# Storing the first tile of a row softmax as two DMAs of eight rows instead of one of sixteen

## The chip, the core and the metric

The kernel runs on one core of a Trainium2 chip. The metric is device time in microseconds (us), the median of several executions. Lower is better.

## The reference

The input x has shape (16, 1024, 512) in float32. For every row of 512 values the kernel computes a softmax at temperature 0.5:

```python
x_scaled = x / 0.5
x_max = np.max(x_scaled, axis=-1, keepdims=True)
exp_x = np.exp(x_scaled - x_max)
out = exp_x / np.sum(exp_x, axis=-1, keepdims=True)
```

There are 16,384 rows, 33.55 MB in and 33.55 MB out.

## The kernel before

The rows are cut into eight tiles ("chunks", c = 0 to 7). A tile has 128 partitions with G = 16 rows of 512 floats each, which is 4 MiB. A partition's 16 rows lie next to each other in HBM, so a DMA of a whole tile is 128 runs of 32 KiB. Six tile buffers exist (BUFS = 6). Tiles 6 and 7 reuse the buffers of tiles 0 and 1, so their loads wait until the stores of tiles 0 and 1 have landed.

All work on a tile is done in place, by blocks of rows that the table BLOCKS lists: tile 0 in blocks of 4, 4 and 8 rows, tiles 1 to 6 whole, tile 7 in two blocks of 8. That makes 11 blocks. For each block:

- shift (L74, L78): VectorE (DVE) takes each row's negated maximum and doubles it, which gives the bias. When the tile has no load yet, this step first issues it (L66) on SyncE's DMA queue (SP). LOADS cuts tile 0's load into 4 and 12 rows; the other tiles are loaded whole.
- exponentials (L85): ScalarE (ACT) computes exp(2x + bias), one instruction per row, and adds up the row's sum.
- scale_vector (L100, L102): DVE takes the reciprocal of the sums and multiplies seven eighths of the block's rows.
- scale_scalar (L111): ACT multiplies the remaining rows.
- store (L119): ACT's queue issues the DMA to HBM. STORES lists the row ranges of each tile's store, and a range is issued with the block whose end is the range's end. Before, every tile is stored whole, after its last block.

The order is written out by hand. The main loop is:

```python
    for i in range(n):
        if i + 1 < n:
            exponentials(i + 1)
        scale_vector(i)
        scale_scalar(i)
        if i + 2 < n:
            shift(i + 2)
        store(i)
```

Two DMA queues carry everything: q1 takes the loads, issued by SP, and q10 takes the stores, issued by ACT. Each DMA is spread over the same 16 DMA engines, eight partitions to each, so one tile's load or store is eight packets of 32 KiB on each engine, and each engine then writes a 4-byte packet for the semaphore. The framework gives the DMAs eight completion semaphores in turn.

Of the kernel before, what the change touches and what calls it, by code (L numbers as in the profile page):

```python
# [1 line left out]

# [4 lines left out]


@with_exitstack
def kernel(  # L10
    ctx: ExitStack,
    tc: tile.TileContext,
    x: bass.AP,
    out: bass.AP,
):
    nc = tc.nc
    fp32 = mybir.dt.float32
    P = nc.NUM_PARTITIONS
    AX = mybir.AxisListType.X
    EXP = mybir.ActivationFunctionType.Exp  # L20
    COPY = mybir.ActivationFunctionType.Copy
    MAX = mybir.AluOpType.max

    D = x.shape[-1]
    xf = x.flatten_outer_dims()
    of = out.flatten_outer_dims()
    N = xf.shape[0]

    G = 16
    C = N // (P * G)
    assert C * P * G == N
    xr = xf.rearrange("(c p g) d -> c p g d", p=P, g=G)
    outr = of.rearrange("(c p g) d -> c p g d", p=P, g=G)
    WHOLE = [(0, G)]
    LOADS = [[(0, 4), (4, G)]] + [WHOLE] * 7
    BLOCKS = [[(0, 4), (4, 8), (8, G)]] + [WHOLE] * 6 + [[(0, 8), (8, G)]]
    STORES = [WHOLE] * 8  # L40
    BMAX = 16
    BUFS = 6

    data = ctx.enter_context(tc.tile_pool(name="data", bufs=BUFS))
    stats = ctx.enter_context(tc.tile_pool(name="stats", bufs=6))

    ctx.enter_context(tc.manual_schedule())


    warm = stats.tile([P, 1], fp32, name="warm", bufs=1)  # L50
    nc.vector.memset(warm, 0.0)  # L51
    nc.scalar.activation(out=warm, in_=warm, func=EXP)  # L52

    chunks = {}
    blocks = [(c, lo, hi) for c in range(C) for lo, hi in BLOCKS[c]]
    n = len(blocks)
    biases, sums, recips = {}, {}, {}

    def load(c):
        if c < BUFS:  # L60
            chunks[c] = data.tile([P, G, D], fp32, name="xt")
        else:
            chunks[c] = chunks[c - BUFS]
        xt = chunks[c]
        for lo, hi in LOADS[c]:
            nc.sync.dma_start(out=xt[:, lo:hi, :], in_=xr[c][:, lo:hi, :])  # L66

    def shift(i):
        c, lo, hi = blocks[i]
        if c not in chunks:  # L70
            load(c)
        b = hi - lo
        negmax = stats.tile([P, BMAX], fp32, name="negmax")
        nc.vector.tensor_reduce(  # L74
            negmax[:, 0:b], chunks[c][:, lo:hi, :], axis=AX, op=MAX, negate=True
        )
        biases[i] = stats.tile([P, BMAX], fp32, name="bias")
        nc.vector.tensor_scalar_mul(biases[i][:, 0:b], negmax[:, 0:b], 2.0)  # L78

    def exponentials(i):  # L80
        c, lo, hi = blocks[i]
        sums[i] = stats.tile([P, BMAX], fp32, name="sums")
        for g in range(hi - lo):
            row = chunks[c][:, lo + g, :]
            nc.scalar.activation(  # L85
                out=row,
                in_=row,
                func=EXP,
                bias=biases[i][:, g : g + 1],
                scale=2.0,  # L90
                accum_out=sums[i][:, g : g + 1],
            )


    def scale_vector(i):
        c, lo, hi = blocks[i]
        b = hi - lo
        k = b - b // 8
        recips[i] = stats.tile([P, BMAX], fp32, name="recip")
        nc.vector.reciprocal(recips[i][:, 0:b], sums[i][:, 0:b])  # L100
        rows = chunks[c][:, lo : lo + k, :]
        nc.vector.tensor_mul(  # L102
            rows, rows, recips[i][:, 0:k].unsqueeze(2).broadcast_to((P, k, D))
        )

    def scale_scalar(i):
        c, lo, hi = blocks[i]
        b = hi - lo
        for g in range(b - b // 8, b):
            row = chunks[c][:, lo + g, :]  # L110
            nc.scalar.activation(  # L111
                out=row, in_=row, func=COPY, scale=recips[i][:, g : g + 1]
            )

    def store(i):
        c, _, end = blocks[i]
        for lo, hi in STORES[c]:
            if hi == end:
                nc.scalar.dma_start(  # L119
                    out=outr[c][:, lo:hi, :], in_=chunks[c][:, lo:hi, :]  # L120
                )

    shift(0)
    shift(1)
    exponentials(0)
# [10 lines that stand above are left out]
# [1 line left out]
_INS = ['x']  # L137
_OUTS = [((16, 1024, 512), 'float32')]


# [23 lines left out]
```

## Time and profile before

| | us |
|---|---|
| median of 5 runs (162.13 to 162.39) | 162.27 |
| the profiled execution, whole | 162.43 |
| its span in the profile | 160.7 |
| DVE busy | 134.6 |
| ACT busy | 102.1 |
| share of the 16 DMA engines' span: q1 (loads) | 49.3% |
| the same: q10 (stores) | 48.4% |

The span runs from the first to the last recorded event of the execution; 1.7 us of the profiled execution's time lie outside it. A queue's share counts the time that its packets took, summed over the 16 engines, against 16 spans. The names L66, L85 and so on are line numbers of the kernel before; the store's line is L119 before and L120 in the changed kernel.

### The profile page before, as it was taken

To read this page: it belongs to the slowest core of one execution; us is meant where nothing else is said; L and a number is where in the kernel's file an instruction comes from. 1 tells how busy PE (TensorE), PEld (TensorE's weight loads), DVE (VectorE), ACT (ScalarE), POOL (GpSimd) and SP (SyncE) were. 2 spreads that over 40 slices of the span, in tenths; PEclk is the share of its full clock that TensorE was granted. 3 is DMA by queue.
4 is the path that set the end of the run, shared out by engine and by line. 5 is a ranking of instruction groups with operands and counts; after the bars stand their busy time and mean duration, and the time that the engine had idled before them with its cause. 6 is when DMAs were issued, how large, how long until landed. Compare 5 with 4: busy or idle time off the path is not lost.

```text
span 160.7 us, 402 instructions
## 1 busy us (share of the span) xinstructions
DVE 134.6 (84%) x45; ACT 102.1 (64%) x273; POOL 0.2 (0%) x4
## 2 busy tenths in 40 slices
DVE  0608999999999999999999999999999999956000
ACT  3072549069979963997299909990999890790000
POOL 0000000000000000000000000000000000000000
DMA  5999999999999999999999999999999999999993
GB/s 192 461 441 473 392 408 506 392 392 516 392 400 383 400 449 457 400 441 465 400 432 465 408 408 483 408 400 490 416 392 490 424 392 457 457 392 449 465 392 139
DMA packets 2450, 67.13 MB, mean 418 GB/s; under 512 B 272, under 2 KB 272, under 8 KB 272
## 3 DMA queue, kind: packets, MB, share of 16 engines
q1 hardware_dynamic: 1296, 33.56, 49.3%
q10 hardware_dynamic: 1152, 33.55, 48.4%
q14 instruction: 2, 0.02, 0.0%
HBM read 33.55 MB, written 33.55 MB: 418 GB/s over the span
## 4 chain that ended last, share of the span: by engine, by line
DVE 80%; DMA 7%; ACT 4%; issue 0%; SPq 0%
DVE negmax L74 42%; DVE xt L102 36%; DMA xt<-in_x_dram 7%; ACT xt L85 4%; DVE bias L78 1%; DVE recip L100 1%; SPq L66 0%
## 5 line engine op out<-in xcount | busy, mean ns | idle before, releaser
L85 ACT ACTIVATE xt<-xt,bias 128x512 f32<-128x512 f32 x128 | 90.4, 707 | 41.5 <-DVE bias L78 41.0
L74 DVE TENSOR_REDUCE negmax<-xt 128x16 f32<-128x8192 f32 (+2 forms) x11 | 69.9, 6353 | 9.3 <-DMA xt<-in_x_dram 9.3
L102 DVE TENSOR_TENSOR xt<-xt,recip 128x7168 f32<-128x7168 f32 (+2 forms) x11 | 62.0, 5637 | 0.4
L85 ACT ACTIVATION_READ_ACCUMULATOR xt<-xt,bias 128x1 f32 x128 | 23.9, 187 | 0.0
L111 ACT ACTIVATE xt<-xt,recip 128x512 f32<-128x512 f32 x15 | 9.9, 706 | 0.0
L100 DVE RECIPROCAL recip<-sums 128x16 f32<-128x16 f32 (+2 forms) x11 | 2.4, 218 | 1.8 <-ACT xt L85 1.8
L78 DVE TENSOR_SCALAR bias<-negmax 128x16 f32<-128x16 f32 (+2 forms) x11 | 1.9, 173 | 0.4
L52 ACT ACT_TABLE_LOAD x1 | 1.3, 1283 | 0.7 <-PEq L148 0.7
L51 DVE MEMSET warm<- 128x1 f32 x1 | 0.1, 59 | 0.8 <-PEq L148 0.8
L52 ACT ACTIVATE warm<-warm 128x1 f32<-128x1 f32 x1 | 0.2, 202 | 0.0
L148 POOL MEMSET const-bfloat16-1.0<- 128x1 bf16 x1 | 0.1, 101 | 0.0
L148 POOL MEMSET const-uint8-127<- 128x1 uint8 x1 | 0.1, 101 | 0.0
L148 POOL MEMSET const-float32-0.0<- 128x1 f32 x1 | 0.1, 98 | 0.2 <-issue 0.2
L148 POOL MEMSET const-float32-1.0<- 128x1 f32 x1 | 0.1, 98 | 0.0
## 6 DMA issues: line engine op xcount, KB each, us to landing
out_dram<-xt ACTq DMA_DIRECT2D x8, 4096.0 KB, 23.1
xt<-in_x_dram SPq DMA_DIRECT2D x7, 4096.0 KB, 30.0
xt<-in_x_dram SPq DMA_DIRECT2D x1, 3072.0 KB, 11.5
xt<-in_x_dram SPq DMA_DIRECT2D x1, 1024.0 KB, 4.6
```

What stands on the lines that cost most here:

```text
L51: nc.vector.memset(warm, 0.0)
L52: nc.scalar.activation(out=warm, in_=warm, func=EXP)
L74: nc.vector.tensor_reduce(negmax[:, 0:b], chunks[c][:, lo:hi, :], axis=AX, op=MAX, negate=True)
L78: nc.vector.tensor_scalar_mul(biases[i][:, 0:b], negmax[:, 0:b], 2.0)
L85: nc.scalar.activation(out=row, in_=row, func=EXP, bias=biases[i][:, g : g + 1], scale=2.0, accum_out=sums[i][:, g : g + 1],)
L100: nc.vector.reciprocal(recips[i][:, 0:b], sums[i][:, 0:b])
L102: nc.vector.tensor_mul(rows, rows, recips[i][:, 0:k].unsqueeze(2).broadcast_to((P, k, D)))
L111: nc.scalar.activation(out=row, in_=row, func=COPY, scale=recips[i][:, g : g + 1])
L148: nc = _bacc.Bacc("TRN2", target_bir_lowering=False, num_devices=1)
```

## The change

Tile 0's entry in STORES becomes two ranges of eight rows. The function store now returns unless the block is the tile's last one, and then issues all of the tile's ranges one after the other. For tiles 1 to 7 nothing changes. Tile 0's store was one DMA with 128 runs of 32 KiB; it becomes two DMAs on the same queue, each with 128 runs of 16 KiB.

```diff
-    STORES = [WHOLE] * 8
+    STORES = [[(0, 8), (8, G)]] + [WHOLE] * 7
...
     def store(i):
         c, _, end = blocks[i]
+        if end < G:
+            return
         for lo, hi in STORES[c]:
-            if hi == end:
-                nc.scalar.dma_start(
-                    out=outr[c][:, lo:hi, :], in_=chunks[c][:, lo:hi, :]
-                )
+            nc.scalar.dma_start(
+                out=outr[c][:, lo:hi, :], in_=chunks[c][:, lo:hi, :]
+            )
```

## The prediction

> **What bounds the kernel now.** I read the page first: the busy shares, the DMA rows and the traffic by slices.
>
> ```profile
> span 160.7 us, 402 instructions
> DVE 134.6 (84%) x45; ACT 102.1 (64%) x273; POOL 0.2 (0%) x4
> DMA  5999999999999999999999999999999999999993
> q1 hardware_dynamic: 1296, 33.56, 49.3%
> q10 hardware_dynamic: 1152, 33.55, 48.4%
> ```
>
> The chain of waits names DVE for 80% of the span, and DVE is busy for 84%. But the two DMA queues together fill 97.7% of the time of all 16 DMA engines. Nothing there can be idle for long, whatever the chain says. So I went to the trace's packet records (start, duration, size of each). On every engine the packets stand end to end from the first at 1.74 us to the last, with no gap over 0.19 us except where the instruction queue puts in a packet. Fifteen engines end between 158.1 and 158.6; one, which also carried two 8 KiB instruction fetches, ends at 159.45, and the last store lands right after it. The kernel is bound by DMA time from end to end. What the engines compute matters only when it makes a queue run dry.
>
> Next I asked for the traffic of stretches around tile 0's store: before it, at its start, beside the loads, and when only stores are left.
>
> ```profile
> DMA packets 297, 8.66 MB, mean 433 GB/s; under 512 B 32, under 2 KB 32, under 8 KB 32
> ...
> DMA packets 48, 1.57 MB, mean 384 GB/s; under 512 B 0, under 2 KB 0, under 8 KB 0
> q1 hardware_dynamic: 32, 1.05, 82.2%
> q10 hardware_dynamic: 16, 0.52, 29.6%
> ...
> DMA packets 291, 8.49 MB, mean 424 GB/s; under 512 B 32, under 2 KB 32, under 8 KB 32
> q1 hardware_dynamic: 147, 4.29, 49.7%
> q10 hardware_dynamic: 144, 4.19, 48.6%
> ...
> DMA packets 440, 12.85 MB, mean 428 GB/s; under 512 B 48, under 2 KB 48, under 8 KB 48
> ```
>
> These are 26 to 46 us, 46.9 to 51, 51 to 71 and 116 to 146. The rate is 424 to 433 GB/s everywhere but in the second stretch. There the queues hold 111.8% of the stretch for 48 packets: the 32 load packets are slow. In the records a 32 KiB packet takes 1213 ns all through the run. When the store queue comes alive, two load packets on each engine take 1.4 to 2.1 us instead, each engine at its own moment. Summed over the two, the excess is 0.78 to 1.15 us per engine, mean 0.945. It happens at no other store or load: after 49.6 us neither queue is ever dry until the loads end, so no other DMA meets a queue that has to start.
>
> The third stretch shows how the two queues share an engine: about one packet each. In the records they alternate strictly, and even the 4-byte semaphore packet takes a turn.
>
> Last, the issues and the waits of the load queue.
>
> ```profile
> 44.65 0.71 ACT L111 ACTIVATE xt<-xt,recip 128x512 f32<-128x512 f32 x1
> 45.39 0.37 ACTq L119 DMA_DIRECT2D out_dram<-xt  x1
> 46.20 0.72 ACT L85 ACTIVATE xt<-xt,bias 128x512 f32<-128x512 f32 x1 [0.84 <-DVE bias L78]
> ...
> 147.35 0.34 ACTq L119 DMA_DIRECT2D out_dram<-xt  x1
> ...
> SPq L66 <- DMA out_dram<-xt: 75.6, 2, 56.7
> ```
>
> The store is issued in a hole of ACT's, and load 6 waits 56.7 us for tile 0's store to land, until 69.4 us.
>
> **The change part by part.** *Issue.* One more DMA on ACT's queue costs 0.34 to 0.37 us there. In the built program the first half waits for nothing (ACT has long seen its rows done), so it can go at about 44.7, under the L111 that the second half waits for. Even were it to follow, 45.39 + 0.37 + 0.34 = 46.10 is short of 46.20, when ACT's next exponential gets its bias. Queued behind it is that exponential alone; cost nothing. Without that hole it would be 0.37 us of ACT, which has 4 to 6 us of idle time per tile. DVE's order does not change.
>
> *Semaphores.* The extra DMA shifts the turn of the eight semaphores. Load 5, which was issued at once, now waits for load 0's first part. That lands at 5.4 us, with some 20 MB still queued ahead of load 5; nothing runs dry. Store 3 waits for the first half of store 0 and store 7 for store 1, both landed long before. Load 6 waits for both halves, load 7 for store 1 as before.
>
> *Packets.* 8 KiB, 24 KiB and 32 KiB packets take 309, 912 and 1213 ns: 37.7 ns per KiB and 8 ns fixed. A 16 KiB packet is then 610 ns, and two are 8 ns more than one of 32 KiB. Eight pairs on each engine plus one more semaphore packet of 9 ns: +0.07 us, on the path in full, as the engines have no gap. The Trainium skill, "DMA: Bandwidth & Descriptors", section on the anatomy of one DMA, speaks against the change: it gives each DMA a fixed cost of about 2.0 us beside its bytes. No such cost shows here: store follows store on q10, and the 24 KiB packets follow the 8 KiB ones, without a gap. By the page's figure the sum would be about 2 us higher.
>
> *The store queue's start.* It cost 0.945 us with 32 KiB packets. The nearest other row is the instruction fetch: 8 KiB, its own 0.31 us and 0.25 and 0.37 us more on the next packet. A line through 0.31 at 8 KiB and 0.945 at 32 KiB gives 0.52 at 16 KiB, a gain of 0.42. If the cost does not depend on the size the gain is zero, if all of it goes the gain is 0.945, and if each half pays for itself it is a loss of 0.945. I take -0.42, as it lies between two measured rows.
>
> *The order of the two queues afterwards.* Turns go by packet, so a store of 16 KiB packets gets a third of an engine, not half. At its first packet nine load packets are left on an engine (one of load 4, eight of load 5). A pair takes 1.213 + 0.610 = 1.823 us, so the loads end near 49.9 + 9 x 1.823 = 66.3 us, where before they ended at 73.5. Seven halves are left: 7 x 0.61 = 4.3, so store 0 ends near 70.6 and lands near 71.3, 2 us later than before. Load 6 is issued then and its first packet comes 1.0 us later (load 0: issued 0.73, first packet 1.74), near 72.4. So the load queue is dry for 6 us. The engines are not: store 0 and store 1, issued at 58.84, fill them. But now the load queue has to start a second time, onto a running queue of 32 KiB packets.
>
> The trace has no row for that start. Its bounds: zero, because the other queue has work and nothing shows that stores suffer as loads do; 0.945, as for the store queue's start with packets of the same size. The load queue's own first start cost 0.47 on average in the first packets, on idle engines. I take 0.945, since that row has the same sizes and two running queues.
>
> The Trainium skill, same page, section on queues and rings, says that an engine goes round its queues by packets and that a packet typically holds some 9 to 17 descriptors. Here the turns change after every single 32 KiB run, eight of which make an engine's part of a store. With the page's packet a half would go out in one turn, the load queue would not run dry, and the sum would be 0.07 - 0.42 = -0.35.
>
> *What is late next.* Load 6 would land near 93 (95.1 before) and DVE reaches tile 6 at 103.8; load 7 lands by 115, DVE reaches it at 120.4. Store 1 ends near 88, as before. At the end, store 7 is issued at 147.35 and can run from about 148.36. That is when the quickest engine comes free, while the engine that sets the end comes free 1.1 us later. So a loss passes to the end in full, and a gain up to about 1.1 us.
>
> **Sum.** 0.07 - 0.42 + 0.945 = +0.59 us. Against the profiled execution, 162.43 + 0.59 = 163.02; the median of the runs lies 0.16 lower, so 162.86. With the bounds of this case, 0.07 - 0.42 + 0.47 = +0.12 to 0.07 + 0 + 0.945 = +1.02: 162.39 to 163.29.
>
> **The rivals.** *The smaller start alone* (faster): the store queue starts more cheaply and the loads' second start costs nothing. 0.07 - 0.42 = -0.35, 161.92; down to 0.07 - 0.945 = -0.88, 161.39, if the start's cost goes altogether. For it: the only slow packets of the trace are at the start that the change touches. Against it: the instruction fetches show that a later start on a running engine costs something too. It decides if the loads' second start costs less than 0.35.
>
> *Nothing but packets* (no change): the start costs the same at any size, and either a second start is free or an engine shares by bytes, so that the load queue never runs dry and the two halves act as one store. +0.07, 162.34. For it: the engines stay full and work is conserved. Against it: the semaphore packet's turn shows sharing by packets.
>
> *Every DMA starts anew* (slower by more): the second half also pays 0.945. 0.07 + 0.945 + 0.945 = +1.96, 164.23. Against it: none of the later stores pays.
>
> **How the numbers follow.** The forecast gets 0.52, the smaller start 0.20, nothing but packets 0.20, every DMA 0.08. About 0.2% (0.32 us) is what a measurement of this kernel can tell from no change. Of the forecast 0.06 lies within it, of the smaller start 0.02. Faster 0.18; same 0.20 + 0.06 + 0.02 = 0.28; slower 0.46 + 0.08 = 0.54. The range from 161.85 to 163.5 takes in the forecast's bounds with some margin, the case without change and the smaller start's own value; the last rival and the smaller start's lower half, together under 0.2, stay out.
>
> **What would show it.** Right: slow load packets near 47 us with a smaller excess, a stretch near 66 to 72 us with packets of q10 alone, load 6 issued near 71, then slow packets on q10. Wrong: load 6 issued at 69 as before (no sharing by packets), no slow packets at the second start, slow packets at each half, or any gap of the engines, above all ahead of store 7.

## The result and the profile after

The changed kernel takes 163.22 us in the median of 22 runs (162.05 to 163.95). The kernel before takes 162.33 us in 41 runs (162.13 to 162.73). The ratio is 1.0052 with a 95% interval of 1.0041 to 1.0062, so the change costs about 0.85 us. Its times are also spread over 1.9 us, where those of the kernel before lie within 0.6 us. The profiled execution below took 162.66 us, which is one of the quicker ones; a slower one, "again", follows.

The page of the changed kernel, answering the first lines shown of before:

```profile
span 160.9 us, 405 instructions
DVE 134.6 (84%) x45; ACT 102.1 (63%) x273; POOL 0.2 (0%) x4
DMA  5999999999989999999899999999999999999993
q1 hardware_dynamic: 1296, 33.56, 49.3%
q10 hardware_dynamic: 1296, 33.56, 48.5%
```

DVE and ACT do what they did. The store queue has 144 packets more (128 for the halves, 16 semaphore writes). The engines stay full. The page therefore shows nothing of the loss; it sits in the length of single packets.

The issues on ACT's queue and load 6 on SP's, from the timeline:

```profile
41.27 0.38 ACTq L120 DMA_DIRECT2D out_dram<-xt  x1
45.51 0.34 ACTq L120 DMA_DIRECT2D out_dram<-xt  x1
46.31 0.72 ACT L85 ACTIVATE xt<-xt,bias 128x512 f32<-128x512 f32 x1 [0.83 <-DVE bias L78]
...
71.86 0.33 SPq L66 DMA_DIRECT2D xt<-in_x_dram  x1
```

The first half goes out at 41.27, when ACT's sequencer reaches it, while ACT itself still works off exponentials. The second goes at 45.51, as the whole store did, and ACT's next exponential has the hole in front of it that it had before (0.84, now 0.83). Load 6 is issued 2.4 us later than before (69.45).

The traffic of 51 to 66 us and of 71.5 to 75.5 us:

```profile
DMA packets 291, 6.37 MB, mean 425 GB/s; under 512 B 32, under 2 KB 32, under 8 KB 32
q1 hardware_dynamic: 146, 4.26, 67.0%
q10 hardware_dynamic: 145, 2.11, 32.9%
...
DMA packets 48, 1.57 MB, mean 393 GB/s; under 512 B 0, under 2 KB 0, under 8 KB 0
q10 hardware_dynamic: 48, 1.57, 91.0%
```

In the first stretch the queues send equal numbers of packets and the stores get a third of the time, as forecast. In the second q1 has no line at all: the load queue is dry. The packet records put its last packet before the pause near 70 and its next at 75.8.

In what follows, **excess** is a packet's time beyond what its size usually takes (309, 611, 912 and 1213 ns for 8, 16, 24 and 32 KiB), summed over a stretch, as a mean over the 16 engines. The **fetch engine** is the engine that also carries the two 8 KiB instruction fetches. It is the last to finish in these profiles (in the first one of the changed kernel by 0.1 us only) and so sets the time. The records don't name an engine; each is followed by its packets, which stand end to end. "Pause" is the longest time for which an engine saw no load packet after 52 us, as a mean over the 16 engines; some 2.4 us are normal, as two packets of a store and the semaphore's turn lie in it.

| kernel | median us | ratio (95%) | pause | excess 15 to 41 us | 41 to 56 | after 56 | last engine ends |
|---|---|---|---|---|---|---|---|
| before | 162.33 | 1 | 2.4 | 0.02 | 0.94 | 0.02 | 159.45 |
| changed | 163.22 | 1.0052 (1.0041 to 1.0062) | 7.7 | 0.02 | 0.80 | 0.44 | 159.63 |
| again (the same kernel) | 163.37 | 1.0061 (1.0039 to 1.0083) | 7.7 | 0.02 | 0.82 | 0.91 | 160.63 |
| touch early | 162.32 | 0.9999 (0.9990 to 1.0008) | 2.4 | 0.02 | 0.86 | 0.02 | 159.18 |
| load 5 halved | 162.46 | 1.0000 (0.9988 to 1.0012) | 2.5 | 0.02 | 0.99 | 0.04 | 159.14 |
| late load 6 | 162.79 | 1.0033 (1.0017 to 1.0048) | 8.1 | 0.02 | 1.01 | 0.44 | 159.92 |
| mid load 6 | 162.47 | 1.0008 (0.9997 to 1.0019) | 3.6 | 0.02 | 1.02 | 0.02 | 159.49 |
| late load 5 | 162.31 | 1.0001 (0.9991 to 1.0011) | 4.8 | 0.02 | 0.79 | 0.04 | 159.54 |
| late both | 162.84 | 1.0029 (1.0016 to 1.0041) | 5.9 | 0.02 | 0.85 | 0.40 | 159.94 |
| halves, late load 5 | 163.19 | 1.0045 (1.0029 to 1.0062) | 5.5 | 0.02 | 0.81 | 0.69 | 160.54 |
| late first half | 162.95 | 1.0035 (1.0023 to 1.0048) | 10.2 | 0.02 | 0.86 | 0.02 | 160.02 |
| early rows | 162.08 | 0.9979 (0.9970 to 0.9987) | 2.5 | 0.53 | 0.30 | 0.01 | 158.95 |

Excess, pause and end come from one profiled execution of each kernel, the median from all its runs.

### The profile page after: what moved, and what is told of

Same layout as the page of the kernel before. It is cut to its first block, busy times and chain, and to the rows that moved or that the text cites. A ratio compares the mean times of both kernels' runs of the same rounds, so it can differ in the third digit from the quotient of the medians.

```text
span 160.9 us, 405 instructions
## 1 busy us (share of the span) xinstructions
DVE 134.6 (84%) x45; ACT 102.1 (63%) x273; POOL 0.2 (0%) x4
## 4 chain that ended last, share of the span: by engine, by line
DVE 80%; DMA 7%; ACT 4%; issue 0%; SPq 0%
DVE negmax L74 42%; DVE xt L102 36%; DMA xt<-in_x_dram 7%; ACT xt L85 4%; DVE bias L78 1%; DVE recip L100 1%; SPq L66 0%
## 5 line engine op out<-in xcount | busy, mean ns | idle before, releaser
L85 ACT ACTIVATE xt<-xt,bias 128x512 f32<-128x512 f32 x128 | 90.4, 707 | 41.6 <-DVE bias L78 41.2
```

The costliest lines, as they stand in the source:

```text
L85: nc.scalar.activation(out=row, in_=row, func=EXP, bias=biases[i][:, g : g + 1], scale=2.0, accum_out=sums[i][:, g : g + 1],)
```

## The experiments

**Again.** The changed kernel, to see a slower execution.

> The changed kernel once more, for another profiled execution and more times. Theory A (the loads' second start): the load queue runs dry near 70 us and comes back near 76 us onto a running store queue; on some engines the first load packet then costs a store packet 0.75 to 0.95 us, on others nothing. The engines that are hit differ from execution to execution, and the time depends on whether the engine that also carries the two instruction fetches is among them: an execution near 163.5 shows that engine hit, one near 162.6 shows it spared. Theory B (packets and pairs of DMAs): nothing is left to chance at 76 us; the same engines lose the same, and slow executions show long or missing time elsewhere. Time +0.89 us over the kernel before, spread over some 1.9 us.

Measured: 163.37 us in the median (162.59 to 164.08); the profiled execution took 163.65. The traffic of 85 to 89 us, in this execution and in the kernel before:

```profile
DMA packets 60, 1.44 MB, mean 360 GB/s; under 512 B 16, under 2 KB 16, under 8 KB 16
q1 hardware_dynamic: 30, 0.98, 74.5%
...
DMA packets 65, 1.61 MB, mean 401 GB/s; under 512 B 16, under 2 KB 16, under 8 KB 16
q1 hardware_dynamic: 32, 1.05, 60.6%
```

Fewer load packets (30 against 32) take more of the engines' time (74.5% against 60.6%). The records show one or two load packets per engine that take 0.5 to 1.2 us too long, on all 16 engines, just before the first packets of store 2. In the first profile five engines lost 0.76 to 0.94 us at 75.9, on a store packet, when the loads came back; a few engines lost up to 0.45 near 87, and nine lost nothing at either place. So the loss is there in both, but its place is not the fixed one that theory A named. The times do follow from the fetch engine. Its excess from the first load to the end, with the fetches, is 2.77 us before, 2.92 in the first profile, 3.92 in this one. With 0.07 for the packets that makes +0.22 and +1.22; the executions took +0.23 and +1.22.

**Late load 6 and touch early.** Store 0 whole; load 6 held back by an instruction that reads its buffer, and the same instruction one tile earlier (i == 3) as a control.

```diff
+    def touch():
+        spot = stats.tile([P, 1], fp32, name="spot", bufs=1)
+        nc.scalar.activation(out=spot, in_=chunks[0][:, 0, 0:1], func=COPY)
...
         store(i)
+        if i == 4:
+            touch()
```

> The kernel before, store 0 whole with 32 KiB packets, and one small ACT instruction that reads tile 0 after the tile 2 scaling, near 75.4 us, so that load 6 can't be issued before that. The load queue is dry from 73.5 us to about 79.5 us, as it is in the changed kernel from 70 to 76, but there is no packet of 16 KiB and no extra DMA. Theory A: the second start alone makes the loss; +0.5 to +1.0 us, with the wide spread of the changed kernel, and store packets 0.75 to 0.95 us too long near 79.5 us on some engines. Theory B: no loss, 162.3, within 0.1 us of the kernel before, and a narrow spread.

> Control for the late load 6: the same small ACT instruction one tile earlier, near 58.8 us, so load 6 still waits only for store 0 and is issued near 69.4 us; the load queue never runs dry. Both theories: as the kernel before, within 0.1 us, narrow spread. A loss here would mean that the instruction itself, or the changed turn of the semaphores, costs something.

Measured: 162.79 us (162.43 to 163.94) and 162.32 us (162.16 to 162.65). A load queue that runs dry beside 32 KiB stores costs time, with the wide spread, and the instruction itself costs nothing. But the excess is not at the restart near 80.7. One engine loses 0.22 us there and the others nothing; 0.43 us come 23 us later, from 101.6 to 105, near the first packets of store 3.

**Load 5 halved.** The changed kernel, with load 5 in two halves as well.

```diff
-    LOADS = [[(0, 4), (4, G)]] + [WHOLE] * 7
+    LOADS = [[(0, 4), (4, G)]] + [WHOLE] * 4 + [[(0, 8), (8, G)]] + [WHOLE] * 2
```

> The changed kernel, store 0 in two halves with 16 KiB packets, and load 5 in two halves of eight rows too. Then eleven of the store's packets meet load packets of their own size, store 0 lands near 68.6 us, load 6 is issued near 69, load 5 ends near 77, and the load queue never runs dry. Theory A: the loss goes; what is left is 0.07 us for each split and the cheaper first start (0.82 us per engine in the changed kernel's profile against 0.97): 162.2 to 162.5, narrow spread. Theory B: the loss stays or grows with the second split, +0.9 us or more.

Measured: 162.46 us (162.09 to 163.02), ratio 1.0000. Load 6 is issued at 68.89, and the load queue never runs dry. The loss of the changed kernel is gone although store 0's packets, the second DMA, the early first half and the shifted semaphores (now by one DMA more) are all still there. This speaks for theory A, and it shows that those four cost nothing where the load queue does not run dry.

**One queue.** All stores on SP's queue, loads 0 to 5 ahead of them, so no second queue ever starts.

```diff
-                nc.scalar.dma_start(
+                nc.sync.dma_start(
...
+    for c in range(BUFS):
+        load(c)
     shift(0)
...
         store(i)
+        if i in (3, 4):
+            load(i + 3)
```

> The kernel before with its stores issued by SP on the loads' queue, the first six loads at the head, load 6 after store 1 and load 7 after store 2 in that queue. Only one queue is left, so none ever starts onto a running one. By theory A the slow load packets near 47 us (0.97 us per engine in the kernel before) are the store queue's start and vanish, and no other takes their place: 161.3 to 161.6, faster by 0.7 to 1.0 us; store 7, issued near 147.3, must not be late. Theory B, and any account in which the first store itself is slow (its first bytes, its first use of the output), keeps 0.9 us of excess where the first store packets run, near 60 us: 162.2 to 162.4.

Measured: 163.75 us (163.50 to 164.17), ratio 1.0094 (1.0078 to 1.0110): slower, where theory A forecast a gain. The traffic from 57.5 to 61.5 us, around the first store packets:

```profile
DMA packets 45, 1.28 MB, mean 319 GB/s; under 512 B 6, under 2 KB 6, under 8 KB 6
q1 hardware_dynamic: 45, 1.28, 98.0%
```

And from 50 to 57 us, ahead of them:

```profile
DMA packets 107, 2.98 MB, mean 426 GB/s; under 512 B 16, under 2 KB 16, under 8 KB 16
```

The engines are held for 98.0% of the first stretch and move 319 GB/s; ahead of it they moved 426. The last one or two load packets before store 0 have an excess of 0.95 us in all, a mean over the engines. So the 0.94 us of the kernel before is not what a queue costs when it starts: it is there, just as large, when the first stores come behind loads on the same queue. The prediction's name for it was wrong. The kernel is slower for its fetch engine, which loses another 0.78 us near 90, on load 6's last packet before store 2, and ends at 160.55; the median engine ends at 158.5, as before (158.4).

**Late load 5, and late both.** Load 5 held back by a small ACT write into its buffer; "late both" adds the touch of the late load 6.

```diff
         for g in range(hi - lo):
+            if i == 4 and g == 10:
+                held.append(data.tile([P, G, D], fp32, name="xt"))
+                nc.scalar.activation(out=held[0][:, 0, 0:1], in_=warm, func=COPY)
...
-            chunks[c] = data.tile([P, G, D], fp32, name="xt")
+            chunks[c] = held[0] if c == 5 else data.tile([P, G, D], fp32, name="xt")
```

> The kernel before with load 5 held back until near 53 us by a small ACT write to its buffer. Load 4 ends near 54, the load queue is dry until near 57, beside a running store queue with packets of 32 KiB; load 6 is issued before load 5 ends, so this is the only second start, 20 us earlier than in the other kernels. Theory A: +0.3 to +1.0 us with a wide spread, as with the late load 6 (+0.45 in the median). If the place or the tile matters and not the dry queue: as the kernel before, 162.3.

> Load 5 held back until near 53 us and load 6 until near 76 us: the load queue runs dry twice beside a running store queue. Theory A: the losses of the two single kernels add up, +0.7 to +1.6 us in the median, with a wide spread. If one disturbance is the whole of it, whatever its number: as one of them alone, near +0.45.

Measured: 162.31 us (162.01 to 162.79) and 162.84 us (162.34 to 163.41). The queues of the late load 5 kernel, from 55 to 57.5 and from 57 to 62 us:

```profile
q10 hardware_dynamic: 32, 1.05, 97.0%
q1 hardware_dynamic: 1, 0.00, 0.0%
...
q1 hardware_dynamic: 32, 1.05, 48.5%
q10 hardware_dynamic: 32, 1.05, 48.5%
```

The load queue is dry (its one packet is a semaphore write), comes back, and the two queues share the engines at once, at full rate: 64 packets in 5 us, none long. Here a dry queue costs nothing, so theory A as I had put it, that each start onto a running queue has its price, has fallen. The two together cost what the late load 6 costs alone, again with excess near 103.

**By partitions.** Two DMAs for store 0, but 32 KiB packets.

```diff
+                for a, z in [(0, 64), (64, P)] if c == 0 else [(0, P)]:
                     nc.scalar.dma_start(
-                        out=outr[c][:, lo:hi, :], in_=chunks[c][:, lo:hi, :]
+                        out=outr[c][a:z, lo:hi, :], in_=chunks[c][a:z, lo:hi, :]
```

> Tile 0's store as two DMAs as in the changed kernel, but cut by partitions (0 to 63 and 64 to 127), so the packets stay at 32 KiB, four and four on each engine, and the two queues share an engine half and half. Store 0 lands near 69.5 us and the load queue never runs dry. Theory A: as the kernel before, 162.2 to 162.5, narrow spread. Theory of the prediction's last rival (every DMA starts anew): +0.9 us. If the second DMA's shift of the semaphores were the cause, the loss of the changed kernel would stay, too.

Measured: 167.13 us (165.32 to 167.81), ratio 1.0273 (1.0235 to 1.0311). This run can't answer its question. Between 54 and 75 us both queues' packets take up to 1.8 us too long, 2.85 us per engine from 56 to 73, store 0 lands only near 76 and load 6 is late for that reason. The Trainium skill, "DMA: Bandwidth & Descriptors", in its rules for kernel authors, advises against two transfers over partition halves since both use the same engines and nothing is won; here it costs 2.7%. Why is not shown.

**Halves, late load 5; mid load 6; late first half.** Three kernels that pull the halves and the dry queue apart. The first is the changed kernel with the edit of the late load 5 (at g == 13). The second is the kernel before with the touch of tile 0 inside tile 3's exponentials (i == 5 and g == 13). The third:

```diff
-        for lo, hi in STORES[c]:
+        for lo, hi in reversed(STORES[c]):
```

> The changed kernel, store 0 in two halves, with load 5 held back until near 55.6 us by a small ACT write. The load queue is then dry from about 55 to 60 us, store 0's halves run alone and land near 61, and load 6 is issued near 62, long before load 5 ends near 79, so the queue does not run dry again. The packets of 16 KiB, the two DMAs and the early first half stay. If any dry load queue beside stores costs time: +0.5 us or more over the kernel before. If what costs is load 6 coming to a dry queue (the late load 5 alone cost nothing): 162.2 to 162.6, narrow spread. If the halves themselves cost time, +0.9 us as in the changed kernel.

> The kernel before with load 6 held back to about 72.4 us, the moment at which the changed kernel issues it, so the load queue is dry from 73.5 to about 76.3 us only, half as long as with the late load 6. If load 6 coming to a dry queue is the cause: +0.3 to +0.9 us, with a wide spread. If the loss needs the halves' packets (the engines out of step with each other) or a long dry stretch: within 0.15 us of the kernel before.

> The changed kernel with the two halves issued in reverse order, so that the first one issued waits for the tile's last rows and both go out near 45.4 us instead of 41.3 and 45.5. If the early first half were part of the loss: nearer to the kernel before than +0.9 us. If the dry load queue is the cause: store 0 starts 4 us later, load 6 is issued later still, near 73 to 74 us, and the loss stays, +0.5 to +1.2 us.

Measured: 163.19 us (162.64 to 163.58), 162.47 us (162.23 to 162.88) and 162.95 us (162.76 to 163.28). The first one's traffic from 64 to 69 us:

```profile
DMA packets 68, 1.64 MB, mean 328 GB/s; under 512 B 16, under 2 KB 16, under 8 KB 16
q1 hardware_dynamic: 33, 1.08, 63.1%
```

Load 5 came back near 60 without loss; 5 us later, where store 0's 16 KiB packets give way to store 1's of 32 KiB, the loads have an excess of about 0.6 us on most engines and 1.65 on the fetch engine. With load 6 at 72.15, almost the moment of the changed kernel (71.86), but 32 KiB packets and a pause of 3.6 us, no loss can be told (ratio 1.0008, 0.9997 to 1.0019). With both halves issued together at 45.25 the loss is there; its profile has no excess at all after the pause of 10 us. What it has is one engine, the fetch engine, with 1.2 us lost on a single step near 52 us (a gap of 0.4 and a load packet 0.76 too long), among 16 KiB store packets. So the loss does not need the early first half. Whether that half adds to it is not shown: 162.95 lies 0.27 us below the changed kernel's 163.22, but the intervals of the ratios overlap (1.0023 to 1.0048 and 1.0041 to 1.0062). The place of the loss wanders between executions and kernels.

**Early rows.** Store 0 cut at row 4, the first part as soon as its rows are ready.

```diff
-    STORES = [WHOLE] * 8
+    STORES = [[(0, 4), (4, G)]] + [WHOLE] * 7
```

> The kernel before with store 0 cut into rows 0 to 3, issued as soon as they are scaled near 17.6 us (8 KiB packets), and rows 4 to 15 at the tile's end (24 KiB). It asks what the 0.97 us per engine near 47 us are, which one queue for everything did not take away. If the first store packets of the execution cost once: excess near 20 us, none near 47 us, time the same or a little lower, 161.9 to 162.4. If stores that begin beside loads cost each time: some 0.3 us near 20 us and 0.8 to 1.0 near 47, 162.5 to 162.8. Load 6 is issued near 68 us, the load queue never runs dry.

Measured: 162.08 us (161.99 to 162.23), ratio 0.9979 (0.9970 to 0.9987). This beats both kernels, by 0.33 us and 1.1 us. The traffic from 46.9 to 51 us:

```profile
DMA packets 49, 1.47 MB, mean 360 GB/s; under 512 B 0, under 2 KB 0, under 8 KB 0
q1 hardware_dynamic: 33, 1.08, 66.6%
```

The 33 load packets take 66.6% of the stretch, where 32 took 82.2% before. The excess is 0.53 us near 20 and 0.30 near 49: split, neither all at the first store nor paid twice in full. For the fetch engine it is 0.17 from 41 to 56 us against 0.94 before, but 0.77 against 0.37 from 15 to 41. From the first load to the end, with the fetches, it is 2.24 against 2.77; with 0.07 for the packets that makes -0.46, and the profiled execution is 0.44 quicker.

## Why the prediction was right, and where it was not

**What bounds the kernel: right.** DVE's busy time is 134.6 us in every run, ACT's 102.0 to 102.4. For the three profiles where I made it (changed, again, early rows), the sum over the fetch engine's packets gives the change of the execution's time to 0.02 us.

**Issue and semaphores: cost nothing, as said.** The first half went out at 41.27, not at 44.7. The trace of before could have told it: ACT's sequencer reached the store at 41.2 and waited there for 3.9 us. By itself it costs nothing: the kernel with load 5 halved has it too, at a ratio of 1.0000.

**Packets: +0.07, as sized.** A 16 KiB packet takes 611 ns (610 forecast). The 2.0 us for each DMA that the prediction set against this term do not show. The Trainium skill, "DMA: Bandwidth & Descriptors", gives them in its section on the anatomy of one DMA for the GpSimd path, and these DMAs are issued by SP and ACT. With load 5 halved there are two DMAs more than before, and the ratio is 1.0000.

**The first stores' cost: mis-sized and misnamed.** The term was -0.42. The excess from 41 to 56 us fell from 0.94 to 0.80 and 0.82 in the two profiles, so -0.13; kernels with whole stores vary from 0.79 to 1.02 there. The line through an instruction fetch and this cost had no ground, and one queue showed that the cost belongs to first stores beside or behind loads, not to a queue's start.

**The order of the queues: right in kind, off in time.** Sharing by packets, store 0's late end and the dry load queue came as described. The loads ended near 70, not 66.3; load 6 was issued at 71.86, not 71.3; its first packet came 4.0 us later, not 1.0. Store 0's own first packet in the kernel before, 4.2 us after its issue, was the row to take, not load 0's on idle engines.

**The second start, +0.945: near in size, for the wrong step.** After 56 us the profiles have 0.44 and 0.91 us of excess that the kernel before has not. Without the dry queue it is gone (load 5 halved). But a short dry spell does not bring it (late load 5, mid load 6), and it need not come at the restart: of the changed kernel's two profiles, the first has long store packets there on five engines (0.76 to 0.94 us), the second hardly any (0.06 to 0.28) and its loss 10 us later; in the other kernels it comes 5 or 23 us later. What the table does show is an order by the length of the pause: the five kernels with 5.5 us or more (changed, late load 6, late both, halves with late load 5, late first half) all lose 0.3 to 0.6%, with 16 KiB store packets or without, and the six with 4.8 us or less lose nothing that can be told, load 5 halved with its 16 KiB packets among them. This is a count of kernels, not a cause: the one profile of the late first half lost its time near 52 us, ahead of its pause. Whether 16 KiB packets make the loss larger, beside a long pause, is not shown either. Apart from the restart in the first profile, it shows near the first packets of a later store, and it is largest on the fetch engine, which runs out of step with the others. What holds the packets up inside an engine is open; the records do not show it.

**The sum.** +0.59 was forecast, about +0.85 measured, inside the range. On the fetch engine, which sets the time, the first stores' term is -0.29 and -0.18 in the two profiles (-0.42 forecast) and the excess after 56 us +0.50 and +1.23 (+0.945 forecast). With 0.07 for the packets these terms make +0.28 and +1.12 of the +0.23 and +1.22 that the two executions took. So the direction came from the step that was argued, the load queue run dry, and load 5 halved bears it out; that the size came within 0.3 us is in part luck, as the price was taken from the first stores, for a step at which the loss need not sit, and the loss itself varies by 1 us between executions. The last bound (a loss passes to the end in full) held; the rivals' cases (a gain, no change, each DMA paying) did not.

## What to carry to other kernels

When the DMA engines are full from end to end, busy shares and gaps no longer tell kernels apart; compare the time of single packets, and follow the one engine that finishes last. The two queues here shared an engine packet by packet (146 packets against 145, 67.0% of the time against 32.9%), so the size of a store's packets decided how much of the engine it got and when its buffer came free. Look at what that does to the other queue: here all kernels whose loads stood still for over 5 us were slower, and halving load 5 as well, so that sizes were equal for longer, took the loss away. A small early store ahead of the large ones was worth 0.2% here; try it before cutting the large one in halves.

## What the runs showed of the hardware

- A DMA issued onto a queue that is empty while the other queue runs shows its first packet about 4 us after the issue (load 6: 71.86 to 75.8; store 0 before: 45.39 to 49.6; 3.5 to 4.4 us in the other kernels), against 1.0 us on idle engines (load 0: 0.73 to 1.74).
- Where the first stores run beside or behind loads, load packets on each engine are held up, 0.8 to 1.0 us in all, whether the stores have a queue of their own or not. With 32 KiB store packets it is one or two load packets of an engine; with a small store sent ahead (early rows) it was 0.53 us at the first store and 0.30 at the second.
- The engine that carries the two 8 KiB instruction fetches ends 1.1 us behind the median engine (159.45 against 158.36 in the kernel before; the fetches take 0.31 us each, and the packets behind them 0.37 and 0.25 too long). In the kernels that lose time it loses up to 1.6 us where most others lose 0.6. In the changed kernel's two profiles the fetch engine's share accounts for the whole difference of 1.0 us.
